# A last layer's sum and norm: Pool taken out, and part of the sum moved into TensorE's accumulation

## The chip, the cores and the metric

One core of a Trainium2 chip runs the whole program once. The metric is the device time of that run in microseconds (us), here the median of three runs of the same compiled kernel. Five engines run their own instruction streams side by side: PE (TensorE, matmuls), DVE (VectorE), ACT (ScalarE), POOL (GpSimd) and SP, which here only issues DMA transfers. They wait for one another by semaphores. Matmul results land in PSUM (eight banks of 512 float32 columns on 128 partitions), everything else is in SBUF or in device memory.

## What is computed

The reference is an encoder of two layers over 1024 tokens of width 1024. Each layer has four sequence mixers, a memory cross-attention and a mixture of experts, each followed by a residual sum and a layer norm. What this change touches is the end of the second layer:

```python
y = sum over the two chosen experts of  gate * expert_output      # (1024, 1024)
x = layer_norm(DN_ALPHA * x + y, ln3_g, ln3_b)                    # DN_ALPHA = 4 ** 0.25
# layer_norm: (x - mean) * rsqrt(var + 1e-5) * g + b, over the 1024 columns of a token
return x
```

Everything is float32.

## The kernel before

The experts of a layer run one after the other in `moe`; each expert's outputs are scattered by token to a table in device memory, `y_d` (one indirect DMA per expert, issued by POOL). When the last expert has been scattered, the second layer ends in `output()` (L2218 to L2252). It works on eight tiles of 128 tokens. For each tile it

- loads the two expert outputs of each token (`y`, L2243, 1 MB; SP issues the DMA),
- forms the gated sum on PE: `dg[:, t, i]` is a diagonal matrix with the gates of expert i, made on ACT ahead of time (L2239), and four float32 matmuls (two column halves, two experts) accumulate `dg @ y` into a PSUM tile `s` of 128x1024, which takes two banks (L2248),
- adds the residual on DVE: `x = ALPHA * x + s` (L2250), where `x` (`xs[t]`) was loaded to SBUF earlier (L2234),
- normalizes `x` (`layer_norm`, L290),
- and stores it (L2252).

`layer_norm` takes the statistics with `bn_stats` over two halves (L296) and `bn_aggr` (L298), adds the epsilon (L300), and gets the inverse root from two ACT steps, Ln and Exp (L283, L284), and one Newton step of three [128x1] instructions on DVE (L285 to L287). For the last part it has two forms. With `spread=None` DVE does two 128x1024 steps (L309, L310). With `spread` set, DVE makes a bias (L303), ACT scales and shifts (L304), the engine named by `spread` multiplies by g (L305) and POOL adds b (L306). The table `COMB[1]` (L802) picks the form for each tile of `output()`: tiles 0, 2, 4, 6 have DVE for the multiplication, tiles 1, 3, 5 have POOL, tile 7 has the form without `spread`. In all of the first seven, POOL adds b.

What sets the order: a scheduler writes each engine's stream ahead of time, and each engine runs its own stream in that order. PSUM tiles `s` come from a pool of three buffers (`cbs`), so the sum of tile t+3 waits until DVE has read tile t. The buffers for `y` are one in `W.right` (tiles 0 and 4) and three in `W.late` (the others), so the loads of tiles 4 to 7 wait until PE has read tiles 0 to 3. SP issues in its own order: a load that stands behind a store waits for that store's data.

Of the kernel before, what the change touches and what calls it, by code (L numbers as in the profile page):

```python
# [13 lines left out]
S = 1024  # L14
# [167 lines left out]
F32 = mybir.dt.float32  # L182
# [3 lines left out]
AF = mybir.ActivationFunctionType  # L186
ALU = mybir.AluOpType
AX = mybir.AxisListType
PSUM = bass.MemoryType.PSUM
DRAM = bass.MemoryType.DRAM  # L190

ALPHA = 4.0 ** 0.25
LN_EPS = 1e-5
# [3 lines left out]
def bcast_row(ap, n):  # L197
    return bass.AP(tensor=ap.tensor, offset=ap.offset, ap=[[0, 128], [1, n]])


class K:
# [88 lines left out]
    def layer_norm(self, x, out, g, b, spread=None, halves=False):  # L290


        V, sm = self.V, self.small
        st = self.t(sm, [128, 2, 6], "st")
        for i in range(2):
            V.bn_stats(st[:, i], x[:, 512 * i:512 * i + 512])  # L296
        mv = self.t(sm, [128, 2], "mv")
        V.bn_aggr(mv, st)  # L298
        r = self.t(sm, [128, 3], "rs")
        V.tensor_scalar(r[:, 0:1], mv[:, 1:2], LN_EPS, None, ALU.add)  # L300
        self.rsqrt(r[:, 0:1], r[:, 1:2], r[:, 2:3])
        if spread is not None:
            V.scalar_tensor_tensor(r[:, 2:3], mv[:, 0:1], -1.0, r[:, 1:2], ALU.mult, ALU.mult)  # L303
            self.S.activation(out=out, in_=x, func=AF.Identity, scale=r[:, 1:2], bias=r[:, 2:3])  # L304
            spread.tensor_tensor(out, out, g, ALU.mult)  # L305
            self.G.tensor_tensor(out, out, b, ALU.add)  # L306
            return
        for n in (slice(0, 512), slice(512, 1024)) if halves else (slice(0, 1024),):
            V.scalar_tensor_tensor(out[:, n], x[:, n], mv[:, 0:1], g[:, n], ALU.subtract, ALU.mult)  # L309
            V.scalar_tensor_tensor(out[:, n], out[:, n], r[:, 1:2], b[:, n], ALU.mult, ALU.add)  # L310

    def transpose_split(self, x, xh, xl, ps, tag="tp"):

        for j in range(2):
            p = self.t(ps, [128, 4, 128], tag)
            for k in range(4):
                c = 4 * j + k
                self.T.transpose(p[:, k], x[:, 128 * c:128 * c + 128], self.ident)  # L318
            h = xh[:, 4 * j:4 * j + 4]
            self.S.activation(out=h, in_=p, func=AF.Copy)  # L320
            self.V.tensor_tensor(xl[:, 4 * j:4 * j + 4], p, h.bitcast(F32), ALU.subtract)  # L321
# [477 lines left out]
SMALL = 0.3  # L799
EMPTY = float(1 << 20)  # L800
NX, NY = 4, 4
COMB = (1, 1, 1, 1, 1, 1, 1, 1), (1, 2, 1, 2, 1, 2, 1, 0)  # L802
RW, SPLIT, ATT, SHARES = 420, 2.13, 1 / 90, (70, 12)
DECAY = math.exp(-0.5)

# [1257 lines left out]
def moe(k, l, x2_d, lg, sl, W):  # L2063
    nc, A, V, S, T, G = k.nc, k.A, k.V, k.S, k.T, k.G
    dma = nc.sync.dma_start
    y_d = k.dt([2048, 1024], "ya")
    with ExitStack() as es:
# [10 lines left out]
        def rows(pt, x):  # L2078
            xh, xl = k.t(pl, [128, 8, 128], "xh", F32R), k.t(pl, [128, 8, 128], "xl", F32R)
            k.transpose_split(x, xh, xl, pt)  # L2080
            return xh, xl
# [6 lines left out]
        def silu(p):  # L2088
            h = k.t(pl, [128, 256], "hh")
            S.activation(out=h, in_=p[:, 0:256], func=AF.Tanh, scale=0.5)  # L2090
            V.scalar_tensor_tensor(h, h, 1.0, p[:, 0:256], ALU.add, ALU.mult)
            V.scalar_tensor_tensor(h, h, 0.5, p[:, 256:512], ALU.mult, ALU.mult)
            return h
# [22 lines left out]
        def psums(es):  # L2116
            return k.pool(es, "eps", 2, PSUM), k.pool(es, "ept", 4, PSUM), k.pool(es, "epy", 1, PSUM)
# [7 lines left out]
        with k.tc.If(nov > 0):  # L2125
            with ExitStack() as es1:
# [4 lines left out]
                with k.tc.For_i(0, nov) as b:  # L2131
                    with ExitStack() as es2:
# [7 lines left out]
                        ps, pt, py = psums(es2)  # L2140
                        buf = xg[NX - 1]
                        gather(buf, ix[:, 0:1])
                        x = rows(pt, buf)
# [8 lines left out]
                        p = k.t(ps, [128, 512], "h")  # L2152
# [6 lines left out]
        ps, pt, py = psums(es)  # L2159
        gather(xg[NX - 1], tok[:, NX - 1:NX])  # L2160
        x, h = rows(pt, xg[0]), None
        for e in range(32):
            p = k.t(ps, [128, 512], "h")
# [7 lines left out]
            x, h = xn, silu(p)  # L2171
# [10 lines left out]
    def combine():  # L2182
        with ExitStack() as es:
# [23 lines left out]
            for t in range(8):  # L2207
# [4 lines left out]
                for i in range(2):  # L2212
                    V.scalar_tensor_tensor(x, y[:, i], gate[:, t, i:i + 1], x, ALU.mult, ALU.add)
                k.layer_norm(x, x, g3, b3, (None, V, G)[COMB[0][t]])
                dma(k.x_d[128 * t:128 * t + 128], x)
                yield t, x

    def output():  # L2218

        with ExitStack() as es:  # L2220
            ps = k.pool(es, "cbs", 3, PSUM)
            cp = k.pool(es, "cbc", 1)
            big = lambda p: k.t(p, [128, 2176 if p is k.raw else 2048], "raw")[:, :2048]
            gb = big(k.raw)
            g3, b3 = (gb[:, i:i + 1024] for i in (0, 1024))
            dma(g3, bcast_row(A["ln3_g"][l], 1024))
            dma(b3, bcast_row(A["ln3_b"][l], 1024))
            xs = []
            for p in (W.left, W.left, W.left, k.raw):
                b = big(p)  # L2230
                for i in (0, 1024):
                    t = len(xs)
                    xs.append(b[:, i:i + 1024])
                    dma(xs[t], x2_d[128 * t:128 * t + 128])  # L2234

            dg = cp.tile([128, 8, 2, 128], F32, name=k.uid("dg"))
            for t in range(8):
                for i in range(2):
                    S.activation(out=dg[:, t, i], in_=k.ident, func=AF.Copy, scale=gate[:, t, i:i + 1])  # L2239
            k.ln_exp()  # L2240
            for t in range(8):
                y = big(W.late if t % 4 else W.right)
                dma(y, y3[t].rearrange("p k n -> p (k n)"))  # L2243
                s = k.t(ps, [128, 1024], "s")
                for c in range(0, 1024, 512):
                    for i in range(2):
                        n = 1024 * i + c
                        T.matmul(s[:, c:c + 512], dg[:, t, i], y[:, n:n + 512], start=(i == 0), stop=(i == 1))  # L2248
                x = xs[t]
                V.scalar_tensor_tensor(x, x, ALPHA, s, ALU.mult, ALU.add)  # L2250
                k.layer_norm(x, x, g3, b3, (None, V, G)[COMB[1][t]])
                dma(k.out[128 * t:128 * t + 128], x)  # L2252

    if l == 1:
        output()
        return iter(())
# [110 lines left out]
```

## Time and profile before

| | us |
|---|---|
| median of three runs (lowest, highest) | 3552.11 (3550.23, 3552.54) |
| the profiled execution | 3550.88 |
| its span, first to last instruction | 3549.1 |
| busy in the span: PE, DVE, ACT, POOL | 3135.7, 2461.7, 1576.2, 694.5 |

The profile is of one execution; times in the rows below count from its first instruction. `output()` is its last stretch of some 70 us. "Busy" counts the time in which an instruction was under way on an engine, also where that instruction was held up. The trace shows a float32 matmul as two passes, each with a row of its own (MATMUL), and the loading of its weights on a row PEld. A time in brackets behind an instruction is how long its engine sat idle before it, with what ended that. Small instructions overlap: the next one on an engine can start before the one ahead of it has ended, so what an instruction costs its engine is the distance of two starts.

### The profile page before, as it was taken

The page shows a single profiled execution, that of the slowest core. Times are in us where ns is not written, and L with a number is a line of the kernel's source. Part 1 is how long each engine was busy: PE and PEld are TensorE (multiplying, and loading weights), DVE is VectorE, ACT ScalarE, POOL GpSimd, SP SyncE. Part 2 cuts the span into 40 slices and gives each one's busy share as a digit, 9 for nine tenths or more (in the row PEclk, how much of TensorE's full clock was granted, in tenths as well). Part 3 has the DMA queues.
Part 4 walks back from the last instruction along what each step waited for, and adds up shares of the span by engine and source line. Part 5 has one row for each costly group of instructions (what it writes and reads, how often), then busy time and mean ns, then how long its engine had stood idle before and what let it go on. Part 6 is the DMA issues. An engine that isn't in the chain of part 4 may idle for free. (4 is left out here: it accounts for less than half of the span.)

```text
span 3549.1 us, 56989 instructions
## 1 busy us (share of the span) xinstructions
PE 3135.7 (88%) x22814; PEld 2382.8 (67%) x22814; DVE 2461.7 (69%) x3844; ACT 1576.2 (44%) x2303; POOL 694.5 (20%) x490
## 2 busy tenths in 40 slices
PE   7989799888879997999599888998888799979995
PEld 7867455467757886777487564554677588857772
DVE  6546786588746466899754577857887464669996
ACT  3344343345432312888434354433454223248882
POOL 0000353420010003322210003534100000043333
PEclk9999798889989997999799997988899899979997
DMA  5223411135365133999542342211444741249994
GB/s 212 105 78 130 109 38 45 38 93 158 112 218 192 50 118 127 339 364 372 201 165 98 95 150 50 55 26 45 130 130 120 261 148 66 95 171 366 365 337 179
DMA packets 270215, 545.71 MB, mean 154 GB/s; under 512 B 90608, under 2 KB 170096, under 8 KB 236400
## 3 DMA queue, kind: packets, MB, share of 16 engines
q1 hardware_dynamic: 244496, 486.31, 40.3%
q0 software_dynamic: 24288, 53.52, 4.3%
q8 instruction: 182, 2.98, 0.3%
q10 hardware_dynamic: 1152, 2.10, 0.2%
q14 instruction: 97, 0.79, 0.1%
HBM read 444.29 MB, written 131.07 MB: 162 GB/s over the span
## 5 line engine op out<-in xcount | busy, mean ns | idle before, releaser
L1688 DVE TENSOR_TENSOR wl<-raw,wh 128x2048 fp32r<-128x2048 f32 x208 | 477.2, 2298 | 71.2 <-ACT wh L1687 70.9
L1687 ACT ACTIVATE wh<-raw 128x2048 fp32r<-128x2048 f32 x216 | 414.0, 1917 | 160.0 <-PE y L260 101.1
L1462 POOL TENSOR_TENSOR acc<-acc,pT 128x512 f32<-128x512 f32 x224 | 308.9, 1399 | 306.4 <-PE o L1457 169.6
L258 PE MATMUL bg<-wh,xh 128*128 128x512 f32 x768 | 311.2, 405 | 31.0 <-ACT xh L1729 31.0
L260 PE MATMUL bg<-wh,xl 128*128 128x512 f32 x768 | 306.2, 399 | 2.6 <-DVE xl L1730 2.5
L259 PE MATMUL bg<-wl,xh 128*128 128x512 f32 x768 | 307.6, 401 | 0.0
L1473 ACT ACTIVATE pT<-b 128x512 f32<-128x512 f32 x224 | 128.1, 595 | 202.9 <-PE b L1471 198.1
L1437 DVE TENSOR_REDUCE nmx<-a 128x1 fp32r<-128x1024 f32 x120 | 146.1, 1218 | 102.1 <-PE a L1430 101.6
L258 PE MATMUL h<-wh,xh 128*128 128x512 f32 x512 | 209.0, 408 | 0.3 <-ACT xh L320 0.3
L730 PE MATMUL p<-xh,wh 128*128 128x512 f32 x640 | 207.4, 403 | 0.9 <-DVE r L580 0.9
L320 ACT ACTIVATE xh<-tp 128x512 fp32r<-128x512 f32 x224 | 123.2, 600 | 186.7 <-PE tp L318 177.5
L260 PE MATMUL h<-wh,xl 128*128 128x512 f32 x512 | 203.9, 398 | 0.0
L259 PE MATMUL h<-wl,xh 128*128 128x512 f32 x512 | 203.2, 397 | 0.0
L730 PE MATMUL p<-xl,wh 128*128 128x512 f32 x640 | 200.0, 391 | 0.0
L730 PE MATMUL p<-xh,wl 128*128 128x512 f32 x640 | 199.3, 391 | 0.0
L258 PEld LDWEIGHTS bg<-wh,xh 128*128 128x128 f32 x768 | 146.1, 190 | 64.7 <-ACT xh L1729 32.7
L2113 POOL DMA_INDIRECT ya<-yo,slot x64 | 96.1, 1501 | 422.6 <-ACT xh L320 135.1
L977 POOL DMA_DIRECT2D xs<-zlo x48 | 26.4, 556 | 768.7 <-DVE raw L523 362.3
L260 PEld LDWEIGHTS bg<-wh,xl 128*128 128x128 f32 x768 | 145.8, 190 | 39.1 <-DVE xl L1730 5.2
L259 PEld LDWEIGHTS bg<-wl,xh 128*128 128x128 f32 x768 | 146.4, 191 | 30.9
L321 DVE TENSOR_TENSOR xl<-tp,xh 128x512 fp32r<-128x512 f32 x224 | 146.3, 683 | 29.7 <-ACT xh L320 29.5
L1688 POOL TENSOR_TENSOR wl<-raw,wh 128x2048 fp32r<-128x2048 f32 x8 | 36.3, 4555 | 600.9 <-DVE sx L1881 301.5
(518 smaller groups left out, 7862.6 us busy)
## 6 DMA issues: line engine op xcount, KB each, us to landing
raw<-in_moe_w_dram SPq DMA_DIRECT2D x192, 1024.0 KB, 10.6
raw<-in_w_inb_dram SPq DMA_DIRECT2D x20, 1024.0 KB, 5.1
x<-x SPq DMA_DIRECT2D x40, 512.0 KB, 3.3
mz<-in_mem_wkv_dram SPq DMA_DIRECT2D x64, 256.0 KB, 3.4
mz<-in_mem_wqt_dram SPq DMA_DIRECT2D x32, 256.0 KB, 3.5
wqk<-rec SPq DMA_DIRECT2D x32, 256.0 KB, 2.6
mz<-in_mem_wo_dram SPq DMA_DIRECT2D x32, 256.0 KB, 3.2
vw<-rec SPq DMA_DIRECT2D x32, 256.0 KB, 3.0
```

What stands on the lines that cost most here:

```text
L258: self.T.matmul(ps, ah, bh, start=start, stop=False)
L259: self.T.matmul(ps, ah, bl, start=False, stop=False)
L260: self.T.matmul(ps, al, bh, start=False, stop=stop)
L320: self.S.activation(out=h, in_=p, func=AF.Copy)
L321: self.V.tensor_tensor(xl[:, 4 * j:4 * j + 4], p, h.bitcast(F32), ALU.subtract)
L730: T.matmul(p[i], a, b[i][:, kk], start=(kk == 0 and a is h and b is xh), stop=(kk == 7 and a is lo))
L1437: V.reduce_max(mx[:, j, t:t + 1], b, axis=AX.X)
L1462: G.tensor_tensor(acc[j], acc[j], p[j], ALU.add)
L1473: S.activation(out=p[j], in_=b, func=AF.Exp, scale=scale)
L1687: k.S.activation(out=h, in_=raw, func=AF.Copy)
L1688: (k.G if pool else k.V).tensor_tensor(lo, raw, h.bitcast(F32), ALU.subtract)
L2113: G.indirect_dma_start(out=y_d, out_offset=bass.IndirectOffsetOnAxis(ap=ai, axis=0), in_=y, in_offset=None, bounds_check=2047, oob_is_err= ...
```

## The change

Three edits, all of them for `output()` in the second layer:

1. `COMB[1]` goes; no tile of `output()` uses ACT's and POOL's form of the norm any more.
2. For tiles 0, 1, 2, 3 and 7 (`own(t)`) the residual is summed on PE: `al` is a diagonal matrix with ALPHA, and two matmuls `al @ x`, one per column half, open the accumulation in `s`; the matmuls on `dg` go on in it. The new `norm_sum` then takes statistics and the first norm step straight from PSUM, in halves of 512 columns (L317, L323), and the last step over 1024 columns in SBUF (L324). Tiles 4, 5 and 6 keep L2250 (now L2281) and take the norm of two DVE steps.
3. The pool of PSUM tiles has four buffers instead of three, and the matmuls on `al` of tiles 0 to 3 are written ahead of the loop.

```diff
+    def norm_sum(self, p, out, g, b):
+        V, sm = self.V, self.small
+        st, mv, r = self.t(sm, [128, 2, 6], "st"), self.t(sm, [128, 2], "mv"), self.t(sm, [128, 3], "rs")
+        for i in range(2):
+            V.bn_stats(st[:, i], p[i])
+        V.bn_aggr(mv, st)
+        V.tensor_scalar(r[:, 0:1], mv[:, 1:2], LN_EPS, None, ALU.add)
+        self.rsqrt(r[:, 0:1], r[:, 1:2], r[:, 2:3])
+        for i in range(2):
+            n = slice(512 * i, 512 * i + 512)
+            V.scalar_tensor_tensor(out[:, n], p[i], mv[:, 0:1], g[:, n], ALU.subtract, ALU.mult)
+        V.scalar_tensor_tensor(out, out, r[:, 1:2], b, ALU.mult, ALU.add)
...
-COMB = (1, 1, 1, 1, 1, 1, 1, 1), (1, 2, 1, 2, 1, 2, 1, 0)
+COMB = (1, 1, 1, 1, 1, 1, 1, 1),
...
-            ps = k.pool(es, "cbs", 3, PSUM)
+            ps = k.pool(es, "cbs", 4, PSUM)
...
+            al = cp.tile([128, 128], F32, name=k.uid("al"))
+            S.activation(out=al, in_=k.ident, func=AF.Copy, scale=ALPHA)
             k.ln_exp()
+            own = lambda t: t < 4 or t == 7
+            ss = {}
+
+            def begin(t):
+                ss[t] = k.t(ps, [128, 1024], "s")
+                for c in range(0, 1024, 512) if own(t) else ():
+                    T.matmul(ss[t][:, c:c + 512], al, xs[t][:, c:c + 512], start=True, stop=False)
+
+            for t in range(4):
+                begin(t)
             for t in range(8):
                 y = big(W.late if t % 4 else W.right)
                 dma(y, y3[t].rearrange("p k n -> p (k n)"))
-                s = k.t(ps, [128, 1024], "s")
+                if t > 3:
+                    begin(t)
+                s, x = ss[t], xs[t]
                 for c in range(0, 1024, 512):
                     for i in range(2):
                         n = 1024 * i + c
-                        T.matmul(s[:, c:c + 512], dg[:, t, i], y[:, n:n + 512], start=(i == 0), stop=(i == 1))
-                x = xs[t]
-                V.scalar_tensor_tensor(x, x, ALPHA, s, ALU.mult, ALU.add)
-                k.layer_norm(x, x, g3, b3, (None, V, G)[COMB[1][t]])
+                        T.matmul(s[:, c:c + 512], dg[:, t, i], y[:, n:n + 512], start=(i == 0 and not own(t)), stop=(i == 1))
+                if own(t):
+                    k.norm_sum((s[:, :512], s[:, 512:]), x, g3, b3)
+                else:
+                    V.scalar_tensor_tensor(x, x, ALPHA, s, ALU.mult, ALU.add)
+                    k.layer_norm(x, x, g3, b3)
                 dma(k.out[128 * t:128 * t + 128], x)
```

PE's stream before, from the experts' last matmul (L260) on; `s` is a sum's PSUM tile, `raw` a buffer with `y`:

```order
L260 MATMUL y_34858<-wh_34775,htl_34855 128x512
L2248 MATMUL s_34922<-raw_34920,dg_34902 128x512 x4
L2248 MATMUL s_34947<-raw_34945,dg_34902 128x512 x4
L2248 MATMUL s_34972<-raw_34970,dg_34902 128x512 x4
L2248 MATMUL s_34997<-raw_34995,dg_34902 128x512 x4
```

And now, with what each waits for (`raw` in the rows on `al` is x; the names in brackets are semaphores, of DMA queues and of engines):

```order
L260 MATMUL y_34858<-wh_34775,htl_34855 128x512
L2264 MATMUL s_34922<-raw_34890,al_34919 128x512 [waits DMAHW3_49,DMAHW2_49,DMAHW6_49,DMAHW1_49,DMAHW7_49,DMAHW0_49,Activation_49]
L2264 MATMUL s_34922<-raw_34890,al_34919 128x512
L2264 MATMUL s_34925<-raw_34890,al_34919 128x512 [waits DMAHW0_49]
L2264 MATMUL s_34925<-raw_34890,al_34919 128x512
L2264 MATMUL s_34928<-raw_34893,al_34919 128x512 [waits DMAHW1_49]
L2264 MATMUL s_34928<-raw_34893,al_34919 128x512
L2264 MATMUL s_34931<-raw_34893,al_34919 128x512 [waits DMAHW2_49]
L2264 MATMUL s_34931<-raw_34893,al_34919 128x512
L2277 MATMUL s_34922<-raw_34934,dg_34902 128x512 [waits DMAHW1_49]
```

Eight matmuls on `al` have come in between; the four tiles' sums are begun, and the matmuls on `dg` follow as before. Tile 7's two stand just ahead of its matmuls on `dg`.

SP's stream before, from the load of tile 4's `y` on (L2243 loads `y`, L2252 stores an output):

```order
L2243 DMA raw_35020<-ya_31691 128x2048
L2243 DMA raw_35045<-ya_31691 128x2048
L2243 DMA raw_35070<-ya_31691 128x2048
L2252 DMA out_dram<-raw_34890 128x1024
L2243 DMA raw_35095<-ya_31691 128x2048
L2252 DMA out_dram<-raw_34890 128x1024
```

And now (L2270 loads, L2283 stores):

```order
L2270 DMA raw_35022<-ya_31691 128x2048
L2283 DMA out_dram<-raw_34890 128x1024
L2270 DMA raw_35045<-ya_31691 128x2048
L2283 DMA out_dram<-raw_34890 128x1024
L2270 DMA raw_35068<-ya_31691 128x2048
L2283 DMA out_dram<-raw_34893 128x1024
L2270 DMA raw_35091<-ya_31691 128x2048
```

Before, only the load of tile 7 stood behind a store; now the loads of tiles 5, 6 and 7 stand behind the stores of tiles 0, 1 and 2.

DVE's stream now, for tile 1 (`s_34925`) with tile 0's last step (L324) and tile 2's `bn_stats` in between:

```order
L317 BN_STATS st_34962<-s_34925 128x6
L324 SCALAR_TENSOR_TENSOR raw_34890<-raw_34890,rs_34942,raw_34887 128x1024
L317 BN_STATS st_34962<-s_34925 128x6
L318 BN_AGGR mv_34963<-st_34962 128x2
L319 TENSOR_SCALAR rs_34964<-mv_34963 128x1
L323 SCALAR_TENSOR_TENSOR raw_34890<-s_34925,mv_34963,raw_34887 128x512
L285 TENSOR_TENSOR rs_34964<-rs_34964 128x1
L323 SCALAR_TENSOR_TENSOR raw_34890<-s_34925,mv_34963,raw_34887 128x512
L286 SCALAR_TENSOR_TENSOR rs_34964<-rs_34964 128x1
L317 BN_STATS st_34984<-s_34928 128x6
L287 SCALAR_TENSOR_TENSOR rs_34964<-rs_34964 128x1
```

Every large step of the norm is on DVE now; ACT has only Ln and Exp left in this stretch, POOL has nothing.

## Rows read from the trace of the kernel before

**Rows 1.** Busy us: length, PE, PEld, DVE, ACT, POOL; clock, DMA share, GB/s.
```profile
3493.75:3540.10 46.35, 24.00 (x56) 10.28 (x54) 45.01 (x77) 11.27 (x23) 21.08 (x9) 0.79 0.44 161
```

**Rows 2.** Waits, 3480 to 3550: us in total, times, longest.
```profile
DVE raw L2250 <- PE s L2248: 19.2, 2, 18.9
```

**Rows 3.** In order of time: start, duration (us); a POOL step and DVE beside it.
```profile
3532.59 2.41 POOL L305 TENSOR_TENSOR raw<-raw,raw 128x1024 f32<-128x1024 f32 x1 [2.82 <-ACT raw L304]
3532.73 2.29 DVE L303 SCALAR_TENSOR_TENSOR rs<-mv,rs 128x1 f32<-128x1 f32 x1
```

**Rows 4.** DVE's groups by line, 3480 to 3549: busy us, mean ns.
```profile
L2250 DVE SCALAR_TENSOR_TENSOR raw<-raw,s 128x1024 f32<-128x1024 f32 x8 | 9.7, 1210 | 19.2 <-PE s L2248 19.2
L286 DVE SCALAR_TENSOR_TENSOR rs<-rs 128x1 f32<-128x1 f32 x8 | 7.8, 975 | 0.1
```

**Rows 5.** DVE in order of time where POOL is still: the norm's steps.
```profile
3127.56 0.74 DVE L309 SCALAR_TENSOR_TENSOR x<-x,mv,g 128x512 f32<-128x512 f32 x1
...
3128.29 0.74 DVE L309 SCALAR_TENSOR_TENSOR x<-x,mv,g 128x512 f32<-128x512 f32 x1
...
3530.50 0.68 DVE L296 BATCH_NORM_STATS2 st<-raw 128x6 f32<-128x512 f32 x1
...
3531.17 0.15 DVE L286 SCALAR_TENSOR_TENSOR rs<-rs 128x1 f32<-128x1 f32 x1
3531.24 0.19 DVE L298 BATCH_NORM_AGGREGATE mv<-st 128x2 f32<-128x12 f32 x1
...
3531.47 0.15 DVE L300 TENSOR_SCALAR rs<-mv 128x1 f32<-128x1 f32 x1
3531.54 1.27 DVE L309 SCALAR_TENSOR_TENSOR raw<-raw,mv,raw 128x1024 f32<-128x1024 f32 x1
```

**Rows 6.** Single microseconds, columns as in rows 1 (granted clock behind POOL).
```profile
3474.00:3475.00 1.00, 0.58 (x3) 0.42 (x4) 0.42 (x1) 0.36 (x2) 0.64 (x1) 1.00 0.00 0
3477.00:3478.00 1.00, 0.48 (x3) 0.05 (x1) 0.00 (x0) 0.48 (x1) 0.00 (x0) 1.00 0.08 33
3479.00:3480.00 1.00, 0.00 (x0) 0.00 (x0) 0.00 (x0) 0.00 (x0) 0.79 (x1) 0.74 0.00 0
3493.00:3494.00 1.00, 1.00 (x4) 0.42 (x3) 0.25 (x1) 0.00 (x0) 0.00 (x0) 0.93 0.57 238
```

**Rows 7.** In order of time: ACT's copies, PE's sums, y loads; landing.
```profile
3473.06 1.02 ACT L2112 ACTIVATE yo<-y 128x1024 f32<-128x1024 f32 x1 [0.52 <-PE y L260]
...
3477.52 1.02 ACT L2112 ACTIVATE yo<-y 128x1024 f32<-128x1024 f32 x1 [3.15 <-PE y L260]
...
3487.00 30.75 PE L2248 MATMUL s<-raw,dg 128*128 128x512 f32 x64 [9.52 <-issue]
...
3493.75 0.32 SPq L2243 DMA_DIRECT2D raw<-ya  x1
...
3497.18 0.32 SPq L2243 DMA_DIRECT2D raw<-ya  x1
...
DMA to landing us min/median/max: 4.7/5.4/10.9
```

**Rows 8.** The slowest of DVE's 512-wide steps of this operation, whole span.
```profile
L1016 DVE SCALAR_TENSOR_TENSOR tmp<-P,kn 128x512 f32<-128x512 f32 x16 | 15.7, 984 | 0.0
```

**Rows 9.** The end: POOL, last store, closing drains (duration in ns).
```profile
3478.82 0.97 POOL L2113 DMA_INDIRECT ya<-yo,slot  x1 [3.48 <-ACT yo L2112]
...
3540.17 2.34 POOL L306 TENSOR_TENSOR raw<-raw,raw 128x1024 f32<-128x1024 f32 x1 [2.74 <-DVE raw L305]
...
L2252 SPq DMA_DIRECT2D out_dram<-raw x1: 332/332/332, 3542.5 to 3542.5; - x1
...
DMA to landing us min/median/max: 2.6/2.6/2.6
...
L2363 SPq DRAIN  x2: 7/10/13, 3545.6 to 3545.7; - x2
L2363 POOLq DRAIN  x1: 8106/8106/8106, 3540.1 to 3540.1; - x1
```

## The prediction, made before the change was run

> **What bounds the kernel now.** I read the page's table of 40 slices first: in the last one PE falls from 9 tenths to 5 and its clock from 9 to 7, so the program's last 89 us are unlike those before. Then busy time by stretch within it, the waits, and its instructions in order of time. The stretch from 3493.75 to 3540.10 is `output()`'s norm: DVE is busy 45.0 of 46.4 us, PE only 24.0, ACT 11.3, POOL 21.1 [rows 1]. The reader is to see that DVE sets the pace from its first instruction there to its last. Ahead of it DVE idles 18.9 us for PE's first sum [rows 2], and PE itself waits 9.5 us for the experts' last outputs to be read back [rows 7]. Behind it POOL does the last add.
>
> DVE's 45 us is not 45 us of work. A [128x1] instruction (L303) that started 0.14 us after a POOL step took 2.29 us and ended with that step [rows 3]; the eight L286 take 975 ns in the mean [rows 4], the one that meets no POOL step 0.15, and the next starts 0.07 after it [rows 5].
>
> **The change, part by part.** The order shows that nothing ahead of `output()` moves, on any engine; so all of it is counted from 3477.5, the end of the experts' last matmul.
>
> *The early sums.* Eight matmuls (four tiles, two halves) now stand between the experts' last matmul and the first one on `dg`. A tile of four such matmuls (eight passes: the trace has 64 for 32) takes 3.43 us at PE's full clock, the distance of the two y loads that PE's reading releases [rows 7]; so two take 1.71, the eight 6.86, and a pass 0.43 (0.853 at half the clock). The four PSUM tiles take all eight banks, and so the last `yo`, which ACT reads from PSUM until 3478.54 [rows 7], has to be out first: 3478.6 to 3485.4. The first y lands at 3487.0 [rows 7], so they are hidden, with 1.6 us to spare. Queued behind their wait are only the matmuls on `dg`, which wait for y anyway. If the cover were gone, it would be PE at its lower clock for all of it (13.7 us, to 3492.3): tile 0 would be done at 3496.0. The matrix `al` is one 128-wide activation on ACT, which two instructions later idles 0.52 us for PE ahead of a 1024-wide one of 1.02 [rows 7]: hidden.
>
> *PE's clock.* PE stopped at 3477.5, the granted clock fell to half (1.2 GHz) at about 3479.5 and came back at about 3493.1, six us after PE started [rows 6]. So tile 0 took from 3487.00 to 3493.75, 6.75 instead of 3.43. Now PE is busy almost until y comes. Pauses of 1.1 us (for `yo`) and 1.6 us are left; over the second from 3474 on, in which PE was busy only 0.58 us, the clock stayed at 1.00 [rows 6]. I take it that it stays: tile 0 is done at 3487.00 + 3.43 + 0.25 for the hand-over to DVE = 3490.7. The 0.25 is what is left of 3493.75 when 7.2 passes go at 0.853 until 3493.15 and 0.8 at 0.43. **Term: 3.1 us earlier.** Bounds: 0 (the clock is down at 3487 as before), or 2.2 later (above).
>
> *DVE's work.* With start-to-start times from rows without POOL [rows 5]: `bn_stats` 0.60, `bn_aggr` to the dependent L300 0.23, small ones 0.07, a 1024-wide step 1.19 to 1.20, a 512-wide one 0.73 with a small one behind it. The step over PSUM and x (L2250) lasts 1.21 in the mean [rows 4], 0.07 less than L309, so 1.13 start to start.
> A tile summed on PE (0 to 3 and 7): two `bn_stats` 1.20, `bn_aggr` and L319 0.30, two 512-wide steps with L285 and L286 1.46, L287 0.07, the last step 1.20: 4.23. One of the others (4 to 6): L2281 1.13, then 1.20, 0.30, 1.19, three small ones 0.21, 1.20: 5.23. Together 5 x 4.23 + 3 x 5.23 = 36.8, and 0.3 where a dependent pair stands alone (tile 0, the last tile). **Term: 46.35 becomes 37.1, 9.3 less.** DVE gets ACT's and POOL's large steps and still does less, since no small instruction waits behind POOL any more and five 1.13 steps over x and s are gone.
> Not shown before is `bn_stats` and the first norm step (20 instructions) with PSUM as their source. From the rows: L2250, which reads PSUM, is no slower than L309, which doesn't; if the 0.07 were PSUM's gain for each of the 20, 1.4 less. Upwards, the slowest 512-wide step of this kind in the trace takes 984 ns in the mean [rows 8] against 740 [rows 5]: 20 x 0.24 = 4.8 more. I take 0, by the nearer row. The Trainium skill (Perfetto Trace Analysis, Optimizing Scalar/DVE Operations) speaks against the change here: about 125 ns of access overhead for a DVE instruction on PSUM, about 60 on SBUF. By it, an estimate, 20 x 65 ns = 1.3 us more, and the result 1.3 later; L2250's row doesn't agree with it.
>
> *Does anything hold DVE up?* PE delivers sums at 3490.7, then 3.43 apart; tile 7 with its own two matmuls of x at 3516.4. DVE, at 4.2 to 5.2 a tile, asks for tile 1 at 3494.0 (0.1 wait), for tile 5 at 3507.7 (PE 3507.8), for tile 6 at 3514, for tile 7 at 3519. PSUM is free in time: tile t+4 needs DVE's second 512-wide step of tile t (3493.7, 3498.3, 3503.0, 3506.5), and PE comes there at 3500.7, 3504.1, 3507.5, 3511.0.
> On SP the y loads of tiles 5, 6, 7 now stand behind the outputs of tiles 0, 1, 2. These are ready at about 3496.0, 3500.9, 3505.1; with 0.4 us for an issue and 5.4 to land [rows 7], y5 to y7 come at 3501.8, 3506.7, 3510.9, ahead of PE's need by 2.3, 0.8 and 1.8. At the longest landing, 10.9 [rows 7], y6 would be late by 4.7 on PE, 2 on DVE. So: hidden, 2 at most.
>
> *The end.* POOL's last add (2.34, with its hand-over 2.4 after DVE's last) goes: **term 2.4.** And there is one more: the last output is issued at 3542.5 and lands 2.6 later, SP is through at 3545.7, but the span goes on to 3549.1. POOL's closing drain began at 3540.13 and took 8.11 us, to 3548.24, 5.7 after POOL's last add [rows 9]. Now POOL's last instruction is the scatter at 3478.8 and its drain lies under the norm. Then the end is DVE's last step, 2.6 to land, 0.6 on SP (3545.1 to 3545.7), 0.85 from the last drain to the span's end (3548.24 to 3549.1), 4.05 in all, where POOL's last add was followed by 6.6. **Term: 2.5**; 0 if another engine holds the barrier as long.
>
> **Sum.** 3.1 + 9.3 + 2.4 + 2.5 = 17.3: DVE's last ends at 3490.7 + 37.1 = 3527.8, the span at 3531.8 instead of 3549.1. The profiled execution took 3550.88, 1.8 over its span, so 3533.6; the median of the runs is 1.2 above that execution, so 3534.8 against it.
>
> **Rivals.**
> 1. *The clock falls in the pause before y* (13%). It did fall 2.0 us after PE stopped at 3477.5; the pause left is 1.6, and a late scatter or a slower y load would lengthen it. Then tile 0 comes between 3491 and 3493.75 and the rest follows: 3536 to 3537.9.
> 2. *The end is held anyway* (10%). That the drain is slow because of POOL's add is read from one instance; its length might belong to the program's end. 3534.8 + 2.5 = 3537.3.
> 3. *PSUM as source is dear* (7%): 0.24 more for each of the 20, 3539.6. For it: no row shows `bn_stats` on PSUM. Against it: L2250.
> 4. *The early sums are not early* (4%): the first of them also waits for several DMA queues. If these ended only with y0, the eight would run from 3487.0, lower clock first, tile 0 be done at 3500.6 and the time be 3544.7. Against it: the first matmul on `dg` waits for a queue once more, which is y's.
> 5. *PE becomes the bound, and it is slower than before* (2%). PE has 68 passes from 3487.0 instead of 64. At the lower clock throughout (0.853 a pass) tile 7 comes at 3545.2; DVE's remaining 8.6 and the 4.05 give a span of 3557.9, 3560.9 in the runs. It decides from a mean pass of 0.72 on: then tile 7 comes at 3536.4 and nothing is won. For it: pauses that pull the clock down, with DVE 0.8 us slower a tile than PE. Against it: PE came back to full clock under the same supply [rows 6].
>
> The forecast itself has 62%, several of the small costs together (3545) 2%. The range 3531.5 to 3539.5 holds the forecast, rivals 1 and 2 and most of 3; its own range is 3533 to 3536.5. What this kernel's measurement can tell from no change is about 0.2%, 7 us: faster 0.94, within it 0.04 (rival 4 by half and the small costs), slower 0.02.
>
> **What would show it.** PE busy with s between 3478.6 and 3485.5, and the clock at 1.00 at 3487; the first `bn_stats` near 3490.7; all L285 to L287 of the last tiles at about 0.15; no wait of DVE for PE over 0.3 after tile 1; DVE's last step ends near 3527.8; POOL's drain over before SP's. It is wrong if DVE's stretch is over 40 us, if the first sum is after 3493, or if the end after DVE's last step is near 6.6.

## The result, and the profile after

| | us |
|---|---|
| changed kernel, median of 8 runs (lowest, highest) | 3526.47 (3518.75, 3537.69) |
| kernel before, beside it on the same chip, 8 runs | 3548.1 (3536.18, 3556.59) |
| ratio, 95% interval | 0.9944 (0.9926 to 0.9961) |
| predicted time, range | 3534.8, 3531.5 to 3539.5 |
| profiled execution of the changed kernel, its span | 3518.75, 3517.0 |

The kernel became faster, and the forecast ratio (3534.8 over the 3552.11 it was counted from, 0.9951) lies inside the interval; but the time itself lies 5 us below the range. Of the runs of the kernel before that are counted below, one of 3584.37 us, at a granted clock of 0.868, is left out.

The two profiled spans differ by 32 us, and half of that is not the change's. The experts' last matmul ends at 3477.5 in the trace of before and at 3461.56 in that of the changed kernel, though the instructions up to there are the same, but for the one small activation on ACT that makes `al`. So the rest, called the tail here, is compared from that matmul on: 71.6 us before (the span of 3549.1 less 3477.5), 55.4 after. That is 16.2 less; the sum of the prediction was 17.3.

PE in order of time; columns: start, duration, then idle time in brackets.

```profile
3461.16 0.40 PE L260 MATMUL y<-wh,htl 128*128 128x512 f32 x1
3462.67 7.13 PE L2264 MATMUL s<-raw,al 128*128 128x512 f32 x16 [1.11 <-ACT yo L2126]
3470.91 4.56 PE L2277 MATMUL s<-raw,dg 128*128 128x512 f32 x10 [1.10 <-DMA raw<-ya]
...
3493.96 5.37 PE L2277 MATMUL s<-raw,dg 128*128 128x512 f32 x8 [2.18 <-DMA raw<-ya]
```

The 16 passes on `al` fill the time in which PE idled 9.5 us before [rows 7]; two pauses of 1.1 us are left. The clock in single microseconds, columns as in rows 1:

```profile
3462.00:3463.00 1.00, 0.33 (x1) 0.30 (x2) 0.00 (x0) 0.62 (x1) 0.10 (x1) 1.00 0.00 0
...
3470.00:3471.00 1.00, 0.09 (x1) 0.09 (x1) 0.00 (x0) 0.00 (x0) 0.00 (x0) 1.00 1.00 410
3474.00:3475.00 1.00, 1.00 (x4) 0.50 (x3) 0.29 (x1) 0.00 (x0) 0.00 (x0) 1.00 1.05 442
```

It stays at 1.00 (2.4 GHz) in both pauses and up to the first sum, where it fell to half before [rows 6]. Now DVE's stretch, from its first instruction there to its last (columns as in rows 1), and its groups by line (busy us, mean ns, idle time before):

```profile
3474.70:3512.92 38.22, 27.60 (x60) 11.53 (x58) 36.73 (x80) 3.25 (x16) 0.00 (x0) 0.90 0.63 233
```

```profile
L323 DVE SCALAR_TENSOR_TENSOR raw<-s,mv,raw 128x512 f32<-128x512 f32 x10 | 7.4, 744 | 0.0
L317 DVE BATCH_NORM_STATS2 st<-s 128x6 f32<-128x512 f32 x10 | 6.8, 688 | 15.8 <-PE s L2277 15.8
...
L296 DVE BATCH_NORM_STATS2 st<-raw 128x6 f32<-128x512 f32 x6 | 3.9, 674 | 0.0
...
L2281 DVE SCALAR_TENSOR_TENSOR raw<-raw,s 128x1024 f32<-128x1024 f32 x3 | 3.7, 1220 | 1.2 <-PE s L2277 1.2
L286 DVE SCALAR_TENSOR_TENSOR rs<-rs 128x1 f32<-128x1 f32 x8 | 1.2, 152 | 0.0
```

The stretch is 38.2 us where it was 46.35 [rows 1]; POOL does nothing in it. L286 takes 152 ns in the mean, 975 before [rows 4]. The 1.2 us at L2281 are DVE's only wait in the stretch: PE's sum of tile 6 was late. PE itself had waited 2.18 us for that tile's y load (the row at 3493.96 above), and its eight passes then took 5.37 us, where eight took 3.60 to 3.70 elsewhere, since the clock had fallen after that pause:

```profile
3495.00:3496.00 1.00, 1.00 (x3) 0.48 (x2) 1.00 (x3) 0.00 (x0) 0.00 (x0) 0.50 0.93 369
```

The end, first in order of time, then the closing drains (durations in ns):

```profile
3511.64 1.28 DVE L324 SCALAR_TENSOR_TENSOR raw<-raw,rs,raw 128x1024 f32<-128x1024 f32 x1
```

```profile
L2394 POOLq DRAIN  x3: 46/118/6927, 3462.7 to 3516.7; - x3
L2394 SPq DRAIN  x3: 7/7/13, 3516.1 to 3516.4; - x3
```

POOL's long drain (6927 ns) now starts at 3462.7 and lies under the norm; in rows 9 it ran from 3540.1 for 8106 ns and held the end. From DVE's last step to the span's end it is 4.03 us, 4.05 forecast.

### The profile page after: what moved, and what is told of

Its sections match the earlier page's. It is cut to its first block, busy times and chain, and to the rows that moved or that the text cites. A ratio compares the mean times of both kernels' runs of the same rounds, so it can differ in the third digit from the quotient of the medians.

```text
span 3517.0 us, 57005 instructions
## 1 busy us (share of the span) xinstructions
PE 3131.4 (89%) x22834; PEld 2375.1 (68%) x22834; DVE 2451.2 (70%) x3847; ACT 1568.8 (45%) x2297; POOL 704.4 (20%) x480
## 5 line engine op out<-in xcount | busy, mean ns | idle before, releaser
L260 PE MATMUL bg<-wh,xl 128*128 128x512 f32 x768 | 307.4, 400 | 2.6 <-DVE xl L1744 2.6
L260 PE MATMUL h<-wh,xl 128*128 128x512 f32 x512 | 204.1, 399 | 0.0
L260 PEld LDWEIGHTS bg<-wh,xl 128*128 128x128 f32 x768 | 146.3, 191 | 38.7 <-DVE xl L1744 4.9
```

The costliest lines, as they stand in the source:

```text
L260: self.T.matmul(ps, al, bh, start=False, stop=stop)
```

## The experiments

The theory: the tail's gain is the sum of four things, POOL out of the norm, a clock that stays up, sums done while PE idled, and POOL's drain out of the way; what the time missed by is variation of the unchanged part. Each kernel below was read by its tail, from the end of the experts' last matmul, which does not depend on how long the program took up to there. Times in us; the first sum is taken at DVE's first instruction on it; y1 or y6 is the y load of tile 1 or 6.

| kernel | first sum after that matmul | DVE's stretch | DVE's last to end | tail |
|---|---|---|---|---|
| before, first and second trace | 16.27, 14.85 | 46.3, 46.4 | 9.0, 9.0 | 71.6, 70.2 |
| POOL out only | 15.75 | 41.5 | 4.0 | 61.3 |
| changed, sums late | 16.68 | 39.7 | 4.0 | 60.4 |
| changed, sums made twice | 14.81 | 39.7 | 4.0 | 58.5 |
| changed, three traces | 13.14, 13.30, 13.37 | 38.2, 36.8, 36.8 | 4.0, 4.0, 4.0 | 55.4, 54.1, 54.2 |
| changed, one POOL add at the end | 13.15 | 36.8 | 6.9 | 56.9 |
| changed, stores on ACT | 13.46 | 36.8 | 4.1 | 54.4 |
| all tiles summed on PE | 13.21 | 35.7 | 4.1 | 53.0 |
| the same, first load split | 12.80 | 36.5 | 4.0 | 53.3 |

All but the kernel before and the changed kernel have one trace each. The times of whole programs do not tell these versions apart: on the same occasion the medians were 3530.4 (POOL out only), 3525.9 (sums late) and 3527.5 (changed), and the intervals of their ratios overlap. So what each part is worth rests on the tails.

**The kernel before against itself.** No edit.

> The kernel before, unchanged, timed against itself. Theory (the miss in microseconds is not the change's): the instructions are the same, and still the stretch up to the end of the experts' last matmul differs from the first trace's 3477.5 us by several us, more PE work at the lower granted clock going with a longer time; from that matmul to the span's end it is 71.6 us again, to 1 us. Ratio within 0.3% of 1, single runs spread over 10 us or more. Rival (the first three runs of before showed the true spread): all runs within 2.5 us of each other, the last matmul's end at 3477 to 3478. Then the 16 us that the changed kernel was ahead of the trace of before by that point would need a cause in the change.

Measured: ratio 0.9990 (0.9976 to 1.0004), single runs from 3529.94 to 3546.86. The kernel before ran 93 times in all, these 12 and 81 others; without the one of 3584 the other 92 lie between 3528.5 and 3556.6, median 3541.8, standard deviation 6.3. The three runs that the prediction was counted from are among the six highest of them. The stretch ahead of the tail, for the two traces of before and then the second and third of the changed kernel (columns as in rows 1):

```profile
0.00:3477.48 3477.48, 3104.91 (x22750) 2369.60 (x22750) 2416.66 (x3767) 1563.92 (x2279) 670.12 (x479) 0.92 0.45 153
```

```profile
0.00:3473.53 3473.53, 3106.80 (x22750) 2369.08 (x22750) 2413.98 (x3767) 1564.95 (x2279) 699.95 (x479) 0.92 0.45 153
```

```profile
0.00:3468.92 3468.92, 3098.05 (x22750) 2363.45 (x22750) 2415.63 (x3767) 1564.35 (x2280) 670.49 (x479) 0.93 0.45 154
```

```profile
0.00:3478.32 3478.32, 3103.33 (x22750) 2367.14 (x22750) 2416.90 (x3767) 1563.93 (x2280) 672.67 (x479) 0.92 0.45 153
```

The same 22750 matmul passes take from 3468.9 to 3478.3 us (3461.6 in the changed kernel's first trace), and the longest of them all is one of the changed kernel: the traces give no sign that anything ahead of the tail got faster by the change, though two and three of them can't exclude a few us. The variation goes with the granted clock: over the 84 of these runs whose mean clock is on record, the correlation of time and clock is -0.87, 2.7 us less for 0.001 more. That the clock is the cause is not shown. Where the tail's clock fell is another part of it (columns as in rows 1; this is the second trace of before):

```profile
3475.00:3476.00 1.00, 0.00 (x0) 0.00 (x0) 0.00 (x0) 0.00 (x0) 0.84 (x1) 1.00 0.00 0
3476.00:3477.00 1.00, 0.00 (x0) 0.00 (x0) 0.00 (x0) 0.00 (x0) 0.00 (x0) 0.53 0.41 156
...
3486.00:3487.00 1.00, 1.00 (x3) 0.40 (x3) 0.00 (x0) 0.00 (x0) 0.00 (x0) 0.85 1.01 426
3487.00:3488.00 1.00, 1.00 (x4) 0.46 (x3) 0.00 (x0) 0.00 (x0) 0.00 (x0) 1.00 1.01 426
```

PE started on y at 3483.06 and was back at full clock after some 3.2 us, where the first trace took six [rows 6]. So its first sum came 1.4 us sooner, and the tail was 70.2: the theory's "to 1 us" was a little too narrow.

**The changed kernel again, twice.** No edit.

> The changed kernel, unchanged, timed once more. Theory: from the experts' last matmul to the span's end 55.4 us again (to 1 us), whatever the time up to that matmul is, which lies anywhere between 3455 and 3480; ratio 0.9925 to 0.997. Rival (the change also shortens what stands ahead of it): the last matmul ends near 3461.6 again, 16 us ahead of before, and the ratio is 0.991 or less.

> The changed kernel once more, beside the version above, on the same chip and against the same runs of before. From the experts' last matmul to the end 54.1 us, or 55.4 where y6 lands late; ratio 0.9945 to 0.9965; before's runs spread over 15 us or more around 3540 to 3548, the granted clock in step with them (about 2.5 us less for 0.001 more clock).

Measured: ratios 0.9955 (0.9939 to 0.9970) and 0.9944 (0.9924 to 0.9963), tails 54.1 and 54.2. y6's lateness comes and goes: SP issued it 23.8, 24.0 and 24.0 us after the last matmul in the three traces, but it landed after some 8.5 us (by the end of PE's wait), 5.5 and 8.0. In the third trace PE waited for it as well:

```profile
3510.51 3.67 PE L2277 MATMUL s<-raw,dg 128*128 128x512 f32 x8 [1.75 <-DMA raw<-ya]
```

Here 1.75 us did not reach DVE, and the 55.4 expected for a late y6 did not come; the first trace's 2.18 did, since there the clock had also fallen, to 0.50 at 3495. Over 22 runs on three occasions the changed kernel's median is 3526.4, 15.4 below the 92 runs of before; against the runs of before beside it on each occasion it is 21.6, 16.5 and 18.8 below.

**POOL out, nothing else.**

```diff
-COMB = (1, 1, 1, 1, 1, 1, 1, 1), (1, 2, 1, 2, 1, 2, 1, 0)
+COMB = (1, 1, 1, 1, 1, 1, 1, 1), (0, 0, 0, 0, 0, 0, 0, 0)
```

> The kernel before, with the last layer's final norm on DVE alone, no sum moved to PE and no matmul ahead of the outputs' arrival. The prediction's terms: first sum of PE 16.3 us after the experts' last matmul as before (the clock still falls); DVE 8 x 5.23 + 0.3 = 42.1 us from there (46.35 before); 4.05 from DVE's last to the span's end, POOL's closing drain being over long before. So 62.4 us from the last matmul to the end, 9.2 less than before, ratio about 0.9974. Rival 2 (the end is held whatever ran on POOL): 64.9 to 65. Rival that the small instructions wait for something else than POOL: DVE's stretch stays at 46 us or more.

Measured: ratio 0.9962 (0.9946 to 0.9979), tail 61.3. DVE's stretch and one of its lines (columns as in rows 1 and rows 4):

```profile
3486.62:3528.14 41.52, 23.99 (x56) 10.26 (x54) 41.29 (x80) 3.25 (x16) 0.00 (x0) 0.81 0.50 189
```

```profile
L286 DVE SCALAR_TENSOR_TENSOR rs<-rs 128x1 f32<-128x1 f32 x8 | 1.1, 144 | 0.0
```

DVE took over ACT's and POOL's large steps and was still 4.8 us sooner through; the end after it is 4.04. The whole tail is 9.6 shorter than the mean of before's two, more than half of the change's gain. This edit takes ACT's large steps away as well as POOL's; that it is POOL that holds DVE's small instructions is seen in the kernel before, in one beside a POOL step alone, which ends with it, and one beside an ACT step alone (start, duration):

```profile
3527.42 2.35 POOL L306 TENSOR_TENSOR raw<-raw,raw 128x1024 f32<-128x1024 f32 x1 [3.83 <-DVE rs L285]
...
3528.53 1.25 DVE L286 SCALAR_TENSOR_TENSOR rs<-rs 128x1 f32<-128x1 f32 x1
...
3531.28 1.24 ACT L304 ACTIVATE raw<-raw,rs 128x1024 f32<-128x1024 f32 x1 [0.96 <-DVE rs L303]
3531.36 0.15 DVE L287 SCALAR_TENSOR_TENSOR rs<-rs 128x1 f32<-128x1 f32 x1
```

**The sums late.** The early `begin(t)` goes; the matmuls on `al` stand behind those on `dg`.

```diff
-            for t in range(4):
-                begin(t)
...
+                    if own(t):
+                        T.matmul(s[:, c:c + 512], al, x[:, c:c + 512], start=False, stop=True)
```

> The changed kernel, but each tile's two matmuls on the residual come behind its four on the outputs, so none is done while the outputs are on their way. Theory: the granted clock falls in the pause as before (to half, until about 6 us after PE starts again), PE has 12 passes for tiles 0 to 3, first sum about 18.2 us after the experts' last matmul; tiles 1 to 3 follow 5.1 us apart, more than DVE's 4.23; from the last matmul to the end about 62.3 us against 55.4, 6.9 more. Rival (the early start buys nothing, the gain is all POOL's): 56.5 us or less.

Measured: tail 60.4, ratio 0.9964 (0.9942 to 0.9985). PE and then the clock:

```profile
3479.33 3.62 PE L2273 MATMUL s<-raw,dg 128*128 128x512 f32 x4 [9.54 <-issue]
3482.78 1.02 PE L2275 MATMUL s<-raw,al 128*128 128x512 f32 x2
```

```profile
3479.00:3480.00 1.00, 0.67 (x1) 0.50 (x2) 0.00 (x0) 0.00 (x0) 0.00 (x0) 0.50 1.04 442
```

The clock is at half when y comes, as in before. Moving the residual's sum to PE without starting it early is worth 0.9 us over POOL out (61.3), by one trace of each, whose clock came back at different times (3.4 us after PE started here, 5.0 there): DVE's work falls by the five L2250 steps, but PE's 12 passes a tile, 5.1 us, then set the pace of the first four tiles. The expected 62.3 was 1.9 too much; 1.5 of it is the clock, which came back sooner than in the first trace of before, as it did in the second.

**The sums made twice.** As the changed kernel, and for tiles 0 to 3 once more behind the matmuls on y, which begin the sum anew, so that the early ones only keep PE busy (tile 7's two stand behind its others as well).

```diff
...
-                        T.matmul(s[:, c:c + 512], dg[:, t, i], y[:, n:n + 512], start=(i == 0 and not own(t)), stop=(i == 1))
+                        T.matmul(s[:, c:c + 512], dg[:, t, i], y[:, n:n + 512], start=(i == 0), stop=(i == 1 and not own(t)))
+                    if own(t):
+                        T.matmul(s[:, c:c + 512], al, x[:, c:c + 512], start=False, stop=True)
```

> The matmuls on the residual of tiles 0 to 3 run early as in the changed kernel, and then once more behind each tile's four on the outputs, which write the sum anew: PE is kept busy while the outputs are on their way, but no work is saved there. It separates the clock from the work. If the early matmuls gain by both: first sum 14.9 us after the experts' last matmul (the changed kernel 13.1 and 13.3, the one with late sums 16.7), sums 5.1 apart, so 58.5 to 59 us to the end (changed kernel 54.1 and 55.4, late sums 60.4). If it is the clock alone: 55 us or less. If it is the work alone: 60 us or more.

Measured: tail 58.5, as expected of both together; ratio 0.9970 (0.9954 to 0.9986).

```profile
3475.36 7.13 PE L2264 MATMUL s<-raw,al 128*128 128x512 f32 x16 [1.11 <-ACT yo L2126]
3483.55 1.98 PE L2277 MATMUL s<-raw,dg 128*128 128x512 f32 x4 [1.05 <-DMA raw<-ya]
```

```profile
3483.00:3484.00 1.00, 0.45 (x1) 0.30 (x2) 0.00 (x0) 0.00 (x0) 0.00 (x0) 1.00 1.10 451
```

The clock alone gives 1.9 us (60.4 to 58.5), by one trace of each; the work that is done early gives another 3.1 to 4.4 (58.5 to 55.4 and 54.1).

**A last instruction on POOL.**

```diff
                 dma(k.out[128 * t:128 * t + 128], x)
+                if t == 7:
+                    G.tensor_tensor(al[:, 0:1], x[:, 0:1], x[:, 1:2], ALU.add)
```

> The changed kernel, with one [128x1] add on POOL behind the last tile's last step. It is needed for nothing and no transfer waits for it. Theory (POOL's closing drain takes until 5.7 us after POOL's last instruction, and the end waits for it): about 6.9 us from DVE's last step to the span's end, 2.9 more than the 4.03 of the changed kernel, POOL's last drain over after SP's. Rival 2 of the prediction (the end's length has to do with the size of POOL's add, or with the end of the program, not with when POOL stopped): 4.0 to 4.4.

Measured, in one run: 6.91 us from DVE's last step (3519.85) to the end. In order of time, then the drains (ns):

```profile
3518.57 1.28 DVE L324 SCALAR_TENSOR_TENSOR raw<-raw,rs,raw 128x1024 f32<-128x1024 f32 x1
...
3520.00 0.19 POOL L2285 TENSOR_TENSOR al<-raw 128x1 f32<-128x1 f32 x1 [47.80 <-DVE raw L324]
```

```profile
L2396 POOLq DRAIN  x3: 46/118/5956, 3520.0 to 3526.5; - x3
L2396 SPq DRAIN  x3: 7/7/13, 3523.0 to 3526.2; - x3
```

The last output has landed and SP is through at 3523.1; the span goes on to 3526.8, because POOL's drain lasts until 5.7 us after an add of 0.19. So it is not the size of POOL's last instruction that counts here but when it stopped.

**Stores on ACT's queue.**

```diff
-                dma(k.out[128 * t:128 * t + 128], x)
+                k.nc.scalar.dma_start(k.out[128 * t:128 * t + 128], x)
```

> The changed kernel, but the eight outputs are issued from ACT's queue, so the loads of tiles 5 to 7 no longer stand behind stores that wait for DVE. Theory (the order on SP's queue made y6 late in the first trace of the changed kernel): y5 to y7 are issued 2 to 3 us earlier against the first sum, DVE waits for PE under 0.3 us after tile 1, 54.1 us from the experts' last matmul to the end. Rival (the loads are late because their bytes share the DMA engines with the stores, whichever queue issues them): y's median landing stays at 6.5 us or more, and DVE waits about 1 us for tile 6 or 7 again, 55 to 55.5 us. Rival (ACT's issues hold up its Ln and Exp): DVE's L285 waits, over 55.5 us.

Measured: tail 54.4, no wait of DVE for PE after the first; ratio 0.9966 (0.9954 to 0.9978). SP's issues, then the landing of the y loads:

```profile
3468.08 19.15 SPq L2270 DMA_DIRECT2D raw<-ya  x8
```

```profile
DMA to landing us min/median/max: 4.8/8.1/10.9
```

Both theories have a part: the median landing is 8.1 us (6.6 and 7.5 in the changed kernel's second and third traces; the first has too few landings on record), as the rival says, but y6 is issued 20.3 us after the last matmul in place of 23.8 to 24.0, and no sum after the first waits for a load. In this one trace it is without the 1.2 us of the changed kernel's first; on the other two it gains nothing.

**All tiles summed on PE.** Stores on ACT as above, and:

```diff
-            own = lambda t: t < 4 or t == 7
+            own = lambda t: True
```

> As the one before, and the residual of all eight tiles is summed on PE, three more than in the changed kernel. DVE 8 x 4.23 + 0.3 = 34.1 us by itself, but PE has 12 passes (5.1 us) for each of the last three, which come then at about 38.6 and 43.7 us for tiles 6 and 7, and DVE waits some 0.3 and 0.9 us for these. Theory: 52.5 us from the experts' last matmul to the end, 1.6 less than the best trace of the changed kernel. Rival (PE's clock falls in one of its pauses, or its passes set the pace from tile 4 on): 54 us or more.

Measured: tail 53.0, ratio 0.9951 (0.9932 to 0.9969). Columns as in rows 1:

```profile
3476.58:3512.28 35.70, 30.81 (x72) 13.30 (x70) 34.74 (x80) 3.24 (x16) 0.00 (x0) 0.97 0.65 254
```

The trace agrees to 0.5 us and is the shortest tail of all, 1.2 below the changed kernel's best two. The ratio's interval holds the changed kernel's, so the runs do not show it as better.

**The first load split.** All tiles on PE, and `y` of tile 0 in two column halves.

```diff
...
+                    for c in (0, 512):
+                        dma(y.rearrange("p (k n) -> p k n", k=2)[:, :, c:c + 512], y3[t][:, :, c:c + 512])
```

> As all_own, and the first tile's outputs are loaded in two halves by columns (512 KB each), so PE can begin on the first half while the second is on its way. Theory: PE starts on the outputs 8.3 us after the experts' last matmul, when its early matmuls end (9.4 before), is not stopped by the second half, DVE's first instruction comes at 12.1 instead of 13.2, and since PE sets the pace from tile 4 on, all of it reaches the end: 51.8 us, 1.2 less than all_own. Rival (both halves land together, at the time of the whole): 53 us or more, the first sum at 13.2 or later. In the ratio neither can be told from all_own (about 0.994 to 0.9955).

Measured: tail 53.3, ratio 0.9948 (0.9932 to 0.9965): a miss. PE, then the landing of the two halves:

```profile
3485.26 3.70 PE L2281 MATMUL s<-raw,dg 128*128 128x512 f32 x8 [0.77 <-DMA raw<-ya]
3489.61 10.57 PE L2281 MATMUL s<-raw,dg 128*128 128x512 f32 x24 [0.65 <-DMA raw<-ya]
```

```profile
DMA to landing us min/median/max: 4.4/4.9/5.4
```

Half the bytes took 4.4 us to land where the whole took 4.8 in the kernel above. PE began 0.4 sooner (9.0 us after the last matmul, 9.4 there) and lost it again waiting for y1.

## Why the prediction was right, and where it failed

- **The early sums and the clock: right.** Forecast 6.86 us for the eight matmuls, 7.13 measured, hidden; the clock stayed up until the first sum in all three traces; first sum 13.2 after the last matmul by the forecast, 13.1 to 13.4 measured. The term of 3.1 is 3.1 against the first trace of before but 1.5 against the second, whose clock came back sooner. Rivals 1 and 4 are out.
- **DVE's work: right.** 37.1 forecast; 38.2, 36.8, 36.8. PSUM as a source costs nothing that counts: `bn_stats` 688 ns from PSUM against 674 from SBUF, the 512-wide step 744 against 740 [rows 5]. Rival 3 is out. The Trainium skill (Perfetto Trace Analysis, Optimizing Scalar/DVE Operations) gives an access overhead of about 125 ns for a DVE instruction on PSUM and about 60 on SBUF. The traces do not show that difference: 14 ns and 4 ns in the two pairs above.
- **What holds DVE up: right by its bound.** "Hidden, 2 at most" was 1.24 once and nothing twice. PE, busy 27.6 of the 38.2 us, does not set the pace (rival 5). The order on SP that the prediction named for a wait is only part of the cause. y6 stood behind a store on SP and was issued 23.8 us after the last matmul, as counted (3500.9 + 0.4 less 3477.5); but it took some 8.5 us to land where the sum had 5.4, and at the half clock PE's passes took 1.77 us longer, which the bound did not have. With the stores on ACT's queue y6 still took 8.4 us; why the landing varies stays open.
- **The end: right.** 2.4 + 2.5 = 4.9 forecast, 9.0 to 4.03 measured, and the kernel with one add on POOL shows the drain at work. Rival 2 is out.
- **The step that failed: "the median of the runs is 1.2 above that execution, so 3534.8 against it", and the range built on it.** The sum was set against one execution and three runs within 2.3 us of each other, and the range took in only the unknown costs of the change. The kernel's own level is 3541.8 over 92 runs, and 17.3 below that is 3524.5; the measured median was 3526.47. Even the eight runs of before beside it, with these three among them, have a median of 3548.1, and 17.3 below that is 3530.8, already under the range. A single run's standard deviation of 6.3 us alone is nearly as wide as the whole range of 8. The prediction did say that 0.2%, 7 us, could not be told from no change, and did not put it into the range of the time.

Open: why the first three runs were so alike and so high. Only 4 of the 92 reach 3552.1, and two of three have to for such a median: under 1% of random draws. So runs close in time may not be independent. And the clock goes with most of the variation, not all: the two traces of before differ by 4 us ahead of the tail at the same mean clock of 0.92.

Where the 16 us came from, by the tails: 9.6 POOL out of the norm and its drain, 0.9 the residual on PE, 1.9 the clock, 3.1 to 4.4 sums done early. The middle two are the least certain: they are differences of single traces, and the time at which the clock came back moved the first sum by 1.4 us between two traces of the same kernel.

## What to carry to other kernels

Before an engine's work is shared out, look at what the sharing does to the small instructions beside it: here DVE did the large steps of three engines alone and was through sooner. Fill the time in which PE waits for a transfer with work that is needed anyway: here it paid twice, by the clock and by the work. And give a predicted time two errors, that of the change and that of the level it is counted from; read a small change in a long program from a mark just ahead of it.

## What the runs showed of the hardware that was not expected

- POOL's closing drain ended 5.7 to 5.8 us after POOL's last instruction in each of these: an add of 2.34 us [rows 9], an add of 0.19 us, or the scatter in the changed kernel (it ends at 3463.9, the drain at 3469.6). In the kernel with one add at the end SP was through at 3523.1, so there, as an estimate from these numbers, an instruction on POOL that ended later than 3517.4 would have lengthened the program; that is some 5 us ahead of the last store's landing.
- In five traces of the two kernels the same 22750 passes took between 3461.6 and 3478.3 us, half a per cent, from one execution to the next.
- With the other loads issued behind it, half of a 1 MB load landed after 4.4 us in one trace, the whole after 4.8 in another: splitting the first load gained 0.4 us.
